# Hybrid decoder step: scan work moved by a step, longer waits on the side chain, and row splits moved beside the second projection

## The chip, the cores and the metric

The kernel runs on one core of a Trainium2 chip. The metric is the device time of one execution in microseconds. The engines are named as the profile names them: PE is TensorE's matmul (PEld its weight load), DVE is VectorE, ACT is ScalarE, POOL is GpSimd, and SP only starts DMAs. One execution of the kernel was profiled; all rows below are from that one.

## What is computed

One step of a hybrid decoder layer: 1024 prompt rows and 8 x 4 sample rows, width 1024. All rows pass one input projection, whose columns feed three branches; the three results (3072 wide) pass one output projection. The reference, cut to the parts that the change touches:

```python
def ssd_scan(x, dt, a, bm, cm, h0):              # branch B, chunks of 128 positions
    acum = jnp.cumsum(dt * a.reshape(SSM_GROUPS, hg), axis=2)
    diff = acum[:, :, :, None] - acum[:, :, None, :]
    decay = jnp.exp(jnp.where(causal, diff, -jnp.inf))
    xdt = x * dt[..., None]
    cb = jnp.einsum('bclgn,bcsgn->bclsg', cm, bm)
    y_diag = jnp.einsum('bclsg,bclsgk,bcsgkp->bclgkp', cb, decay, xdt)
    to_end = jnp.exp(acum[:, :, -1:] - acum)
    chunk_states = jnp.einsum('bclgn,bclgk,bclgkp->bcgkpn', bm, to_end, xdt)
    chunk_decay = jnp.exp(acum[:, :, -1])
    def step(h, inp):
        s_c, d_c = inp
        return h * d_c[..., None, None] + s_c, h
    h_final, h_prev = lax.scan(step, h_init, ...)
    y_off = jnp.einsum('bclgn,bcgkpn,bclgk->bclgkp', cm, h_prev, jnp.exp(acum))
    y = (y_diag + y_off)
    ...
def memory_kv(mem, mem_norm_g, w_mem_k, w_mem_v): # 256 memory rows
    m = rmsnorm(mem, mem_norm_g)
    k = jnp.einsum('bmd,de->bme', m, w_mem_k)
    v = jnp.einsum('bmd,de->bme', m, w_mem_v)
    ...
mixed = jnp.concatenate([a_out, b_out, c_out], axis=-1)
y = x + jnp.einsum('bte,ed->btd', mixed, w_out)
```

The scan's output `y` is gated by SiLU of `z`, normed over each group of 512 columns, and is then branch B's result.

## The kernel before

**Products and the side chain.** Nearly all PE work is products of fp32 data split in two: a high part H, rounded by ACT, and the rest L, subtracted by DVE or POOL (`split`, L120 on). `gemm3` issues three matmuls for each 128-deep piece (L339 to L341) and then calls `hook()`. `hook` adds `pace["rate"]` to a counter and advances the *side chain* (a Python generator, its `yield`s are the steps) whenever the counter passes one. So a rate of 0.56 issues a side step after about every second piece. The instruction streams are written out in the order of these calls; there is no scheduler. Every engine runs its own stream in order.

A *unit* is a 2 x 2 block product of 1024 x 1024 pieces done with seven products (B11, T1, T2, B21, T3, B22, T4); at each product's end DVE combines the result out of PSUM (`u`, `gx`, `go`, L508). PSUM banks for side work come from a ring of four (`sd`, L356).

**Stages in order.** The input projection runs in units; beside the units for q, for the memory gate (`mg`) and for the gMLP gate (`gg`) runs the first side chain: sample convolution, `mem_prep` (norm and transposition of the 256 memory rows), the sample scan, the sample scores and values of the attention, the preparation of gMLP's weights. The `u` units follow. Then come two more units and the first output projection (rows of branch A, added to `y_d`), with the scan of the prompt rows as side chain. Then the *key stage* (L2099 to L2119): sixteen products of the memory rows with the key and value weights. In it the rows of branch B (`yb`) are loaded by SP (`loadB`) and split into `bH`, `bL` (`splitB`). Then the second output projection (`outproj(bH, bL)`) with the attention on the side, and the third.

**The scan.** `scan()` has 16 blocks: two groups g, eight chunks c each, and the state `hT` goes from chunk to chunk. A block has five steps.
1. `sA(i+1)`: for the next block C·B^T and the transposed B (PSUM bank psb), the transposed x, then on DVE `cbm` (masked C·B^T, one buffer), ACT `BH`, DVE `BL`, and `xdt`, `xsD`, `xde`. Then `sE(i+1, 0)`: a product (L1228) of `Lt` and `Rt` gives the exponents of four heads, ACT's Relu and Exp make `MT`.
2. `sNorm`; the state product `pst` (three matmuls, L1273 to L1275: BH, BL, xdH, xdL); the product `po` of the state with C (L1217 to L1219: hH, hL, CH, CL); `sM(i+1, 0)`: `MT` times `cbm` on DVE; `t` on DVE; `hT` times decay on POOL (L1287).
3. Four heads of `pd` (L1292, `MT` with `xdt`); DVE `hT` + `pst` (L1297), `xsD` + `t`; ACT `hH`.
4. Four more heads; `sXsplit(i+1)`: `xdH` on ACT, `xdL` on POOL; `sE(i+1, 1)`, which also calls `r_rows(i + 4)`: a DMA issued by POOL that refills one 32-row quarter of `Rt` from `acc_d`; `sC(i+1)`: `CH` on ACT, `CL` on DVE.
5. Transposition of the block before (`y_T`); `sM(i+1, 1)` on POOL; DVE `xsD` + `pd`, `gate_norm` (DVE, then ACT's Square into `sz`, then POOL's `rstd`, L287 and L288); DVE `hL`; four ACT copies (L1138).

Both decay products read the whole tile `Rt`, so that a refill stands between the reader ahead of it and the next.

**Row splits.** `ytodo` lists the rows (g, c) of branch B; (1, 4) to (1, 7) were kept in SBUF, the others are read from `yb_d`:

```python
    ytodo = [(1, c) for c in range(KEEP, 8)] + [(0, c) for c in range(NTILE)] + [(1, c) for c in range(KEEP)] + [(1, 8)]
    def splitB(lag=1):
        if len(ybs) > lag or (ybs and not ytodo):
```

At most three tiles are open at a time; after each product of the key stage one row tile is split and one loaded, after each fourth product two; what is left at the end is split before the next stage.

Of the kernel before, what the change touches and what calls it, by code (L numbers as in the profile page):

```python
# [19 lines left out]
NTILE = 9  # L20
# [38 lines left out]
def hybrid_step(ctx, tc, x_prompt, x_sample, mem_prompt, state_ssm, state_conv, cache_mem_k,  # L59
# [1161 lines left out]
    def sE(i, j):  # L1221

        s_ = S[i]
        if j == 0:
            s_.MT = []
        s_.MT.append(SC_.p.tile([128, 4, 128], F32, tag="MT", name="MT", bufs=3))
        ps = sd()
        PE.matmul(out=ps, lhsT=Lts[i], rhs=SB_.Rt[:, 4 * j:4 * j + 4, :].rearrange("p h l -> p (h l)"), start=True, stop=True)  # L1228
        if j:
            Lts.pop(i)  # L1230
            r_rows(i + 4)
        E = s_.MT[j].rearrange("p h l -> p (h l)")
        ACT.activation(out=E, in_=ps, func=AF.Relu, scale=-1.0)
        ACT.activation(out=E, in_=E, func=AF.Exp, scale=-1.0)
# [12 lines left out]
    def scan():  # L1247
# [12 lines left out]
        for i in range(16):  # L1260
# [8 lines left out]
            if i > 0:  # L1269
                sNorm(i - 1)  # L1270
                sz_load(i)
            pst = sd()
            PE.matmul(out=pst, lhsT=s_.BH, rhs=s_.xH, start=True, stop=False)  # L1273
            PE.matmul(out=pst, lhsT=s_.BL, rhs=s_.xH, start=False, stop=False)
            PE.matmul(out=pst, lhsT=s_.BH, rhs=s_.xL, start=False, stop=True)  # L1275
            if c > 0:
# [8 lines left out]
            if c > 0:  # L1285
                DVE.tensor_tensor(out=h3(t1), in0=h3(po), in1=hb(ea[:, c, hs], 128, 8), op=ALU.mult)
                POOL.tensor_tensor(out=h3(hT), in0=h3(hT), in1=hb(dec[:, c, hs], 128, 8), op=ALU.mult)  # L1287
            yield
            pd = sd()
            for h in range(8):  # L1290
# [14 lines left out]
            if nx:  # L1305
                sXsplit(i + 1)
                sE(i + 1, 1)
                sC(i + 1)
            yield
            if i > 0:  # L1310
                p = S.pop(i - 1)
                gp_, cp_ = divmod(i - 1, 8)
                r = y_T(p.xsD, 128, gp_, cp_ * 128, acc_bank())
            if nx:
                sM(i + 1, 1)
            DVE.tensor_tensor(out=s_.xsD, in0=s_.xsD, in1=pd, op=ALU.add)
# [7 lines left out]
            if i > 0:  # L1324
                fs.append(y_T2(r, 128, gp_, cp_ * 128, sz))
            yield
            for f in fs:
                f()
# [29 lines left out]
    def sample_scan(sp2):  # L1358
# [87 lines left out]
        def s1(b):  # L1446
            hbt = hb_t.pop(b)
            hTb = [sp2.tile([128, 512], F32, tag="hTb", name="hTb", bufs=3) for _ in range(2)]
            for j in range(2):
                ps = sd()  # L1450
                for i in range(4):
                    PE.transpose(out=ps[:, i * 128:(i + 1) * 128], in_=hbt[:, 4 * j + i, :], identity=ident)
                ACT.activation(out=hTb[j], in_=ps, func=AF.Copy)
            Bm = sp2.tile([96, 2, 128], F32R, tag="Bm", name="Bm", bufs=2)
            POOL.tensor_scalar(out=Bm.rearrange("p g n -> p (g n)"), in0=rb(B3), scalar1=bm3[:, b:b + 1], scalar2=None,
                               op0=ALU.mult)
            for k in range(8):
                ACT.activation(out=hbt[:, k, :], in_=hbt[:, k, :], func=AF.Copy, scale=decT[:, k, b:b + 1])
            St[b] = (hbt, hTb, Bm)

        def s2(b, j):
            hbt, hTb, Bm = St[b]
            if j == 0:
                for g in range(2):
                    PE.matmul(out=accs[32 * g:32 * g + 32, :], lhsT=Cm[:, g, b * 32:(b + 1) * 32],
# [28 lines left out]
        f()  # L1494
        set_pace(1.15)
        sz_s = sp2.tile([128, 8, 128], F32, tag="hb", name="sz_s", bufs=4).rearrange("p k n -> p (k n)")[:32]
# [68 lines left out]
    def sample_scores(sap):  # L1565
# [6 lines left out]
                         in_=qs.rearrange("p k (b t) -> p k b t", t=4))  # L1572
        for _ in range(11):
            yield
# [34 lines left out]
        scores(*prev)  # L1609
        set_pace(1.15)  # L1610
        yield
# [10 lines left out]
    def sample_values(sap):  # L1622
# [26 lines left out]
        DVE.tensor_copy(out=Psm, in_=psO)  # L1649
        set_pace(1.15)  # L1650
        yield
# [13 lines left out]
    def mem_prep(p):  # L1665
# [5 lines left out]
        for i in range(2):  # L1671
            mt = p.tile([128, D], F32, tag="mem", name="mem", bufs=2)
            SP.dma_start(out=mt, in_=mem_prompt[0, i * 128:(i + 1) * 128, :])
            mts.append(mt)
        for _ in range(10):
            yield
        rs = []
        for i in range(2):
# [3 lines left out]
            rs.append(r)  # L1682
            for _ in range(3):
                yield
# [96 lines left out]
    def conv_end():  # L1781
# [3 lines left out]
        pace["acc"] = 0.0  # L1785
        set_pace(1.15)

# [204 lines left out]

    def outproj(H, L):
        units = [(ct, b) for ct in range(8) for b in range(3)]
# [11 lines left out]
        for i, (ct, b) in enumerate(units):  # L2006
            t0, n = TB[b]
            if b == 0:
                (wts[ct],) = w_take(1)
            y_open(i + 1)  # L2010
            ps = gemmA(wts[ct], H, L, t0, n)
            t = yt.pop(i)
# [53 lines left out]
    ybp = yb_ctx.enter_context(tc.tile_pool(name="ybp", bufs=1, side="right"))  # L2066
    ytodo = [(1, c) for c in range(KEEP, 8)] + [(0, c) for c in range(NTILE)] + [(1, c) for c in range(KEEP)] + [(1, 8)]

# [29 lines left out]
    n = 0  # L2098
    for blk in range(8):  # L2099
        wp = w_take(2)  # L2100
        cs = slice((blk % 4) * 256, (blk % 4) * 256 + 256)
        for i in range(2):
# [8 lines left out]
            else:  # L2111
                split(ps[:, :256], vH[:, i, cs], vL[:, i, cs], ACT, DVE)
            splitB()
            loadB()
            if n % 4 == 3:
                splitB()
                loadB()
            n += 1
    side.drain()  # L2119
    while ytodo or ybs:  # L2120
        loadB()
        splitB()
    m_ctx.close()
    yb_ctx.close()
    a_ctx = ExitStack()
# [142 lines left out]
    set_pace(0.43)  # L2268
    outproj(bH, bL)
    side.drain()  # L2270
# [173 lines left out]
```

## Time and profile before

| what | value |
|---|---|
| median of three runs | 1353.83 us (1351.43 to 1354.08) |
| the profiled execution's own time | 1354.25 us |
| its span | 1352.5 us |
| mean granted clock of PE in it | 0.977 |
| busy: PE, PEld | 1284.3 us (95%), 1081.3 us (80%) |
| busy: DVE, ACT, POOL | 754.5 (56%), 586.0 (43%), 349.3 us (26%) |
| DMA | 204.67 MB, mean 151 GB/s |

PE's idle time is about a twentieth of the span; the view of waits lists it by the line that waited and by what ended the wait. The granted clock is given by window: 1.00 is full speed, 0.50 half of it. On the span's scale the memory norm runs around 380 us, the sample steps from 480 to 660, the scan from 785 to 1030, the key stage from 1034 to 1096.

### The profile page before, as it was taken

To read this page: it belongs to the slowest core of one execution; us is meant where nothing else is said; L and a number is where in the kernel's file an instruction comes from. 1 tells how busy PE (TensorE), PEld (TensorE's weight loads), DVE (VectorE), ACT (ScalarE), POOL (GpSimd) and SP (SyncE) were. 2 spreads that over 40 slices of the span, in tenths; PEclk is the share of its full clock that TensorE was granted. 3 is DMA by queue.
4 is the path that set the end of the run, shared out by engine and by line. 5 is a ranking of instruction groups with operands and counts; after the bars stand their busy time and mean duration, and the time that the engine had idled before them with its cause. 6 is when DMAs were issued, how large, how long until landed. Compare 5 with 4: busy or idle time off the path is not lost.

```text
span 1352.5 us, 22010 instructions
## 1 busy us (share of the span) xinstructions
PE 1284.3 (95%) x8211; PEld 1081.3 (80%) x8211; DVE 754.5 (56%) x1258; ACT 586.0 (43%) x1227; POOL 349.3 (26%) x384
## 2 busy tenths in 40 slices
PE   8999999999989989999999978889899889999996
PEld 7999998777867667666788756567678889999996
DVE  6112446999855464433467656776664646653543
ACT  6322333645335633221287545555555533322322
POOL 4400624222543221121145232533230000000122
PEclk9999999999999999999899998899899899999998
DMA  7233331333365556374556565234524876657542
GB/s 239 74 88 95 138 92 42 100 106 108 113 195 158 173 153 224 98 260 128 156 164 188 181 199 160 90 97 130 184 81 149 238 217 202 184 178 257 180 137 99
DMA packets 210621, 204.67 MB, mean 151 GB/s; under 512 B 28124, under 2 KB 176688, under 8 KB 209492
## 3 DMA queue, kind: packets, MB, share of 16 engines
q1 hardware_dynamic: 210004, 203.15, 48.3%
q8 instruction: 65, 1.06, 0.3%
q14 instruction: 40, 0.33, 0.1%
q0 software_dynamic: 512, 0.13, 0.1%
HBM read 138.70 MB, written 64.52 MB: 150 GB/s over the span
## 4 chain that ended last, share of the span: by engine, by line
PE 75%; DVE 8%; DMA 6%; ACT 6%; issue 3%; POOL 1%; SPq 1%; POOLq 0%; ACTq 0%; DVEq 0%
PE ps_mm L339 20%; PE ps_mm L340 18%; PE ps_mm L341 18%; DMA yb<-yb_d 1%; PE ps_acc L1645 1%; PE ps_acc L1583 1%; PE ps_sd L1845 1%; DVE ul L457 1%; PE ps_sd L1598 1%; ACT sz L1138 1%; PE ps_sd L1292 1%; DMA sz<-z_d 1%; DVE xsD L1118 1%; PE ps_sd L317 1%; PE ps_sd L490 1%
## 5 line engine op out<-in xcount | busy, mean ns | idle before, releaser
L449 ACT ACTIVATE uh<-wst 128x512 fp32r<-128x512 f32 x80 | 50.1, 626 | 95.6 <-PE ps_mm L340 89.4
L457 DVE TENSOR_TENSOR ul<-wr,uh 128x512 fp32r<-128x512 f32 x84 | 69.5, 828 | 33.5 <-ACT uh L449 33.5
L2349 POOL TENSOR_TENSOR xres<-xres,gfin 128x1536 f32<-128x1536 f32 (+3 forms) x6 | 14.4, 2397 | 282.8 <-DVE ys L2397 241.7
L127 DVE TENSOR_TENSOR wl<-wr,wh 128x512 fp32r<-128x512 f32 (+3 forms) x53 | 51.1, 987 | 61.5 <-ACT wh L124 60.9
L449 ACT ACTIVATE uh<-wr 128x512 fp32r<-128x512 f32 x84 | 52.4, 624 | 64.6 <-PE ps_mm L340 63.0
L457 DVE TENSOR_TENSOR ul<-wst,uh 128x512 fp32r<-128x512 f32 x80 | 61.1, 764 | 26.4 <-ACT uh L449 26.0
L339 PE MATMUL ps_mm<-bH,wh 128*128 128x384 f32 (+1 forms) x192 | 63.4, 330 | 0.0
L341 PE MATMUL ps_mm<-bH,wl 128*128 128x384 f32 (+1 forms) x192 | 62.1, 323 | 0.0
L340 PE MATMUL ps_mm<-bL,wh 128*128 128x384 f32 (+1 forms) x192 | 62.0, 323 | 0.0
L435 POOL TENSOR_TENSOR wst<-wr 128x512 f32<-128x512 f32 x20 | 26.0, 1299 | 133.1 <-DMA wr<-in_w_in_dram 55.3
L124 ACT ACTIVATE wh<-wr 128x512 fp32r<-128x512 f32 (+3 forms) x60 | 47.0, 814 | 23.2 <-PE ps_mm L340 14.0
L339 PE MATMUL ps_mm<-xB22H,uh 128*128 128x512 f32 x128 | 53.2, 416 | 2.9 <-ACT sz_s L1120 2.1
L1016 DVE SCALAR_TENSOR_TENSOR ps_sd<-raw,vecs,ps_sd 128x512 f32<-128x512 f32 x72 | 54.2, 753 | 1.7
L339 PE MATMUL ps_mm<-xT1H,uh 128*128 128x512 f32 x128 | 53.4, 417 | 0.0
L339 PE MATMUL ps_mm<-xB21H,uh 128*128 128x512 f32 x128 | 53.3, 416 | 0.0
L339 PE MATMUL ps_mm<-xB11H,uh 128*128 128x512 f32 x128 | 52.5, 410 | 0.0
L340 PE MATMUL ps_mm<-xB21L,uh 128*128 128x512 f32 x128 | 51.3, 401 | 0.0
L341 PE MATMUL ps_mm<-xB21H,ul 128*128 128x512 f32 x128 | 51.3, 400 | 0.0
L341 PE MATMUL ps_mm<-xT1H,ul 128*128 128x512 f32 x128 | 50.9, 397 | 0.0
L340 PE MATMUL ps_mm<-xT1L,uh 128*128 128x512 f32 x128 | 50.7, 396 | 0.0
L340 PE MATMUL ps_mm<-xB22L,uh 128*128 128x512 f32 x128 | 50.7, 396 | 0.0
L341 PE MATMUL ps_mm<-xB22H,ul 128*128 128x512 f32 x128 | 50.6, 396 | 0.0
(528 smaller groups left out, 4255.5 us busy)
## 6 DMA issues: line engine op xcount, KB each, us to landing
wr<-in_w_in_dram SPq DMA_DIRECT2D x56, 512.0 KB, 4.1
wr<-in_w_out_dram SPq DMA_DIRECT2D x24, 512.0 KB, 4.9
kv<-in_cache_mem_k_dram SPq DMA_DIRECT2D x16, 512.0 KB, 7.1
kv<-in_cache_mem_v_dram SPq DMA_DIRECT2D x16, 512.0 KB, 4.9
xt<-in_x_prompt_dram SPq DMA_DIRECT2D x8, 512.0 KB, 8.4
z_d<-gt SPq DMA_DIRECT2D x32, 128.0 KB, 1.8
v_d<-gt SPq DMA_DIRECT2D x32, 128.0 KB, 3.7
xc_d<-cd SPq DMA_DIRECT2D x16, 256.0 KB, 2.0
```

Of the source, the lines that this page charges most:

```text
L124: ACT.activation(out=H, in_=raw, func=AF.Copy)
L127: leng.tensor_tensor(out=L, in0=raw, in1=rb(H), op=ALU.subtract)
L317: PE.transpose(out=ps[:, i, :T], in_=self.xn[:T, k * 128:(k + 1) * 128], identity=ident[:T, :T])
L339: PE.matmul(out=ps, lhsT=lH, rhs=rH, start=(first and k == k0), stop=False)
L340: PE.matmul(out=ps, lhsT=lH, rhs=rL, start=False, stop=False)
L341: PE.matmul(out=ps, lhsT=lL, rhs=rH, start=False, stop=(last and k == k0 + kn - 1))
L435: POOL.tensor_tensor(out=t1, in0=A_(u, 2, 1), in1=A_(u, 2, 2), op=ALU.add)
L449: ACT.activation(out=h, in_=src, func=AF.Copy)
L457: eng.tensor_tensor(out=l, in0=src, in1=rb(h), op=ALU.subtract)
L490: PE.matmul(out=ps[32 * j:32 * j + 32, 0:256], lhsT=xs[:, 4 * r + j, :], rhs=R[r][:, j, :], start=(r == 0), stop=(r == 1), tile_position=( ...
L1016: DVE.scalar_tensor_tensor(out=ps, in0=raw[:, 512 * h + j:512 * h + j + 512], scalar=cw(ct, j), in1=ps, op0=ALU.mult, op1=ALU.add)
L2349: eng.tensor_tensor(out=t[:, 0:nf, c0:c0 + w], in0=t[:, 0:nf, c0:c0 + w], in1=gc.unsqueeze(1).to_broadcast([128, nf, w]), op=ALU.mult)
```

## The change

Six edits.
- *Scan, state product.* `pst` moves from the second step to the head of the third; `po` stays in the second.
- *Scan, second decay.* `sC(i+1)` comes right after `sXsplit(i+1)` in the fourth step; `sE(i+1, 1)` moves to the fifth; `sM(i+1, 1)` moves behind it to the start of the next block, behind `rstd` on POOL.
- *Scan, strip rows.* `r_rows` is called in `sE(i, 0)` for block i + 3, and no longer in `sE(i, 1)` for i + 4.
- *Sample scan.* Of eight ACT scalings four move from `s1` to `s2`; the pace between the slow stretches is 1.25, not 1.15, in four places.
- *Waits.* `mem_prep` waits 17 steps for its rows instead of 10, then 5 instead of 3 between the two halves; the scores wait 15 instead of 11.
- *Row splits.* `ytodo` goes by column for the first four columns of both groups. In the key stage the first four products are followed by a load and a split at once; products 4 to 14 by a split of a tile that two others stand behind, and a load; the last by two splits and a load. Four row tiles are split in the second output projection, before its first three units (`b_late`).

```diff
@@ sE
         if j:
             Lts.pop(i)
-            r_rows(i + 4)
+        elif i > 0:
+            r_rows(i + 3)
@@ scan
-            pst = sd()
-            PE.matmul(out=pst, lhsT=s_.BH, rhs=s_.xH, start=True, stop=False)
-            PE.matmul(out=pst, lhsT=s_.BL, rhs=s_.xH, start=False, stop=False)
-            PE.matmul(out=pst, lhsT=s_.BH, rhs=s_.xL, start=False, stop=True)
             if c > 0:
...
             yield
+            pst = sd()
+            PE.matmul(out=pst, lhsT=s_.BH, rhs=s_.xH, start=True, stop=False)
+            PE.matmul(out=pst, lhsT=s_.BL, rhs=s_.xH, start=False, stop=False)
+            PE.matmul(out=pst, lhsT=s_.BH, rhs=s_.xL, start=False, stop=True)
             pd = sd()
...
                 sXsplit(i + 1)
+                sC(i + 1)
+            yield
+            if nx:
                 sE(i + 1, 1)
-                sC(i + 1)
-            yield
             if i > 0:
...
-            if nx:
-                sM(i + 1, 1)
             DVE.tensor_tensor(out=s_.xsD, in0=s_.xsD, in1=pd, op=ALU.add)
...
             yield
+            if nx:
+                sM(i + 1, 1)
             for f in fs:
                 f()
@@ sample scan
-            for k in range(8):
+            for k in range(4):
                 ACT.activation(out=hbt[:, k, :], in_=hbt[:, k, :], func=AF.Copy, scale=decT[:, k, b:b + 1])
...
             if j == 0:
+                for k in range(4, 8):
+                    ACT.activation(out=hbt[:, k, :], in_=hbt[:, k, :], func=AF.Copy, scale=decT[:, k, b:b + 1])
...
-        set_pace(1.15)
+        set_pace(1.25)
@@ sample_scores
-        for _ in range(11):
+        for _ in range(15):
             yield
@@ mem_prep
-        for _ in range(10):
+        for _ in range(17):
             yield
...
-            for _ in range(3):
+            for _ in range(5):
                 yield
@@ row splits
-    ytodo = [(1, c) for c in range(KEEP, 8)] + [(0, c) for c in range(NTILE)] + [(1, c) for c in range(KEEP)] + [(1, 8)]
+    ytodo = ([(1, c) for c in range(KEEP, 8)] + [(g, c) for c in range(4) for g in range(2)] +
+             [(0, c) for c in range(4, NTILE)] + [(1, 8)])
...
-            splitB()
-            loadB()
-            if n % 4 == 3:
-                splitB()
+            if n < 4:
+                loadB()
+                splitB(0)
+            elif n < 15:
+                splitB(2)
+                loadB()
+            else:
+                splitB(0)
+                splitB(0)
                 loadB()
...
-    while ytodo or ybs:
-        loadB()
-        splitB()
     m_ctx.close()
-    yb_ctx.close()
...
-    outproj(bH, bL)
+    def b_late(i):
+        if i < 2:
+            for _ in range(2):
+                splitB(0)
+                loadB()
+        elif i == 2:
+            while ytodo or ybs:
+                loadB()
+                splitB(0)
+            yb_ctx.close()
+    outproj(bH, bL, b_late)
```

What stands on DVE around the memory norm (`xn` is the normed memory row tile, `u`, `gx`, `go` the combinations at a unit's product ends, `ul` low parts of weights). Before:

```order
L457 TENSOR_TENSOR ul<-wr,uh 128x512
L309 SCALAR_TENSOR_TENSOR xn<-mem,rstd,mg_b 128x1024
L481 TENSOR_REDUCE sr<-ps_sd 128x64
L457 TENSOR_TENSOR ul<-wst,uh 128x512
L309 SCALAR_TENSOR_TENSOR xn<-mem,rstd,mg_b 128x1024
L508 TENSOR_TENSOR u<-ps_mm,m_4111 128x512
L508 TENSOR_TENSOR gx<-ps_mm,u 128x512
```

Both norm instructions stand ahead of `u`, which the next product on PE waits for. The same stretch of DVE in the changed kernel:

```order
L457 TENSOR_TENSOR ul<-wr,uh 128x512
L481 TENSOR_REDUCE sr<-ps_sd 128x64
L457 TENSOR_TENSOR ul<-wst,uh 128x512
L508 TENSOR_TENSOR u<-ps_mm,m_4111 128x512
L508 TENSOR_TENSOR gx<-ps_mm,u 128x512
L457 TENSOR_TENSOR ul<-wst,uh 128x512
L309 SCALAR_TENSOR_TENSOR xn<-mem,rstd,mg_b 128x1024
L508 TENSOR_TENSOR go<-ps_mm,m_4111 128x512
L457 TENSOR_TENSOR ul<-wr,uh 128x512
L309 SCALAR_TENSOR_TENSOR xn<-mem,rstd,mg_b 128x1024
```

The norm instructions now stand behind `u` and `gx`.

On ACT one block of the scan reads as follows before (L1233 is the second decay's Relu, L1120 the Square):

```order
L1303 ACTIVATE hH<-hT 128x512
L124 ACTIVATE xdH<-xde 128x512
L1233 ACTIVATE MT<-ps_sd 128x512
L1234 ACTIVATE MT<-MT 128x512
L124 ACTIVATE CH<-bc 128x128
L1120 ACTIVATE sz,ss<-xsD 128x512
```

And in the changed kernel (line numbers are one higher from L1233 on):

```order
L1304 ACTIVATE hH<-hT 128x512
L124 ACTIVATE xdH<-xde 128x512
L124 ACTIVATE CH<-bc 128x128
L1234 ACTIVATE MT<-ps_sd 128x512
L1235 ACTIVATE MT<-MT 128x512
L1120 ACTIVATE sz,ss<-xsD 128x512
```

`CH` moved ahead of the Relu and the Exp.

On POOL one block of the scan before (L955 is the refill of `Rt`, L1238 the second mask product, L287 and L288 `rstd`):

```order
L1287 TENSOR_TENSOR hT<-hT,dec 128x512
L127 TENSOR_TENSOR xdL<-xde,xdH 128x512
L955 DMA Rt<-acc_d 2x1024
L1238 TENSOR_TENSOR MT<-MT,cbm 128x512
L287 TENSOR_SCALAR rstd<-ss 128x1
L288 TENSOR_TENSOR rstd<-rstd,mhalf 128x1
```

And in the changed kernel:

```order
L1284 TENSOR_TENSOR hT<-hT,dec 128x512
L127 TENSOR_TENSOR xdL<-xde,xdH 128x512
L287 TENSOR_SCALAR rstd<-ss 128x1
L288 TENSOR_TENSOR rstd<-rstd,mhalf 128x1
L1239 TENSOR_TENSOR MT<-MT,cbm 128x512
L955 DMA Rt<-acc_d 2x1024
```

The mask product and the refill moved behind `rstd`.

## Rows read from the trace of the kernel before

**Rows 1.** Waits of PE: line waited for; us in total, times, longest.
```profile
PE ps_sd L1217 <- DVE BL L127: 12.3, 9, 2.6
PE ps_sd L1228 <- DMA Rt<-acc_d: 8.0, 3, 4.1
PE ps_mm L339 <- ACT wh L124: 6.7, 2, 3.4
PE ps_mm L339 <- DVE u L508: 4.4, 1, 4.4
...
PE ps_sd L1228 <- ACT sz L1120: 2.3, 1, 2.3
...
PE ps_mm L339 <- ACT sz_s L1120: 2.1, 1, 2.1
PE ps_sd L1598 <- DMA kv<-in_cache_mem_k_dram: 2.1, 1, 2.1
```

**Rows 2.** Windows: us; busy PE, PEld, DVE, ACT, POOL; PEclk; DMA; GB/s.
```profile
385.22:388.62 3.40, 3.40 (x11) 2.72 (x10) 2.07 (x4) 0.17 (x1) 1.69 (x2) 0.50 0.51 167
504.69:508.09 3.40, 3.40 (x22) 1.70 (x21) 1.02 (x2) 1.59 (x4) 0.00 (x0) 0.50 0.97 342
...
sum 27.00, PE 22.51 PEld 14.40 DVE 21.00 ACT 13.84 POOL 8.76; mean PE 4.50 PEld 2.88 DVE 4.20 ACT 2.77 POOL 1.75
...
sum 10.10, PE 8.44 PEld 8.15 DVE 7.77 ACT 7.22 POOL 0.00; mean PE 4.22 PEld 4.07 DVE 3.89 ACT 3.61 POOL 0.00
```

**Rows 3.** Timeline, memory norm: start, us, instruction [idle before, its releaser].
```profile
378.66 1.06 ACT L303 ACTIVATE xn<-mem 128x1024 f32<-128x1024 f32 x1 [4.46 <-DMA mem<-in_mem_prompt_dram]
...
384.92 0.51 PE L339 MATMUL ps_mm<-xT3H,uh 128*128 128x512 f32 x1 [4.44 <-DVE u L508]
```

**Rows 4.** Timeline of one block of the scan, four engines.
```profile
933.85 0.29 DVE L127 TENSOR_TENSOR BL<-ps_sd,BH 128x128 fp32r<-128x128 f32 x1 [1.33 <-ACT BH L124]
...
939.25 1.29 POOL L127 TENSOR_TENSOR xdL<-xde,xdH 128x512 fp32r<-128x512 f32 x1 [4.84 <-ACT xdH L124]
...
941.18 1.28 POOL L1238 TENSOR_TENSOR MT<-MT,cbm 128x512 f32<-128x512 f32 x1
...
941.32 1.29 DVE L127 TENSOR_TENSOR CL<-bc,CH 128x128 fp32r<-128x128 f32 x1 [2.79 <-ACT CH L124]
...
944.57 0.63 ACT L1120 ACTIVATE sz<-xsD 128x512 f32<-128x512 f32 x1 [2.76 <-DVE xsD L1118]
...
945.65 0.56 POOL L288 TENSOR_TENSOR rstd<-rstd,mhalf 128x1 f32<-128x1 f32 x1
...
946.66 0.29 DVE L127 TENSOR_TENSOR BL<-ps_sd,BH 128x128 fp32r<-128x128 f32 x1 [1.33 <-ACT BH L124]
...
947.01 0.51 PE L1217 MATMUL ps_sd<-hH,CH 128*128 128x512 f32 x1 [1.60 <-DVE BL L127]
```

**Rows 5.** Tiles CL and Rt: ns min/median/max, first and last start; us to landing.
```profile
L127 DVE TENSOR_TENSOR CL<-bc,CH x14: 293/1286/1972, 804.1 to 1013.2; 128x128 fp32r<-128x128 f32 x14
...
L955 POOL DMA_DIRECT2D Rt<-acc_d x16: 518/635/803, 780.4 to 953.9; - x16
...
DMA to landing us min/median/max: 1.9/2.3/5.0
```

**Rows 6.** Timeline, key stage: product ends on PE, a split on ACT.
```profile
1039.60 0.27 PE L2091 MATMUL ps_sd<-ident,kst 128*128 128x128 f32 x1
...
1042.69 0.27 PE L2091 MATMUL ps_sd<-ident,kst 128*128 128x128 f32 x1
...
1068.13 0.63 ACT L124 ACTIVATE bH<-yb 128x512 fp32r<-128x512 f32 x1 [4.22 <-DMA yb<-yb_d]
```

**Rows 7.** DMA, 1050 to 1100: GB/s in 40 slices; issues, KB, median us to landing.
```profile
GB/s 174 343 359 308 267 141 262 345 346 304 343 325 325 263 82 14 0 112 311 74 321 354 193 270 141 235 345 329 233 74 12 64 260 169 251 340 275 298 199 297
DMA packets 18974, 11.70 MB, mean 234 GB/s; under 512 B 1646, under 2 KB 18971, under 8 KB 18971
...
yb<-yb_d SPq DMA_DIRECT2D x11, 256.0 KB, 5.4
```

More of the change, by code (lines that the diff above doesn't have):

```diff
@@ L1306, in scan @@
                 sXsplit(i + 1)
-                sE(i + 1, 1)
                 sC(i + 1)
             yield
+            if nx:
+                sE(i + 1, 1)
             if i > 0:
@@ L1609, in sample_scores @@
         scores(*prev)
-        set_pace(1.15)
+        set_pace(1.25)
         yield
@@ L1649, in sample_values @@
         DVE.tensor_copy(out=Psm, in_=psO)
-        set_pace(1.15)
+        set_pace(1.25)
         yield
@@ L1785, in conv_end @@
         pace["acc"] = 0.0
-        set_pace(1.15)
+        set_pace(1.25)
     U.bank = sd
@@ L1991, in hybrid_step, with outproj @@
     TB = [(0, 384), (384, 384), (768, 288)]
-    def outproj(H, L):
+    def outproj(H, L, late=None):
         units = [(ct, b) for ct in range(8) for b in range(3)]
@@ L2010, in outproj @@
             y_open(i + 1)
+            if late is not None:
+                late(i)
             ps = gemmA(wts[ct], H, L, t0, n)
```

## The prediction, on record before the changed kernel ran

> **What bounds the kernel now.** I read the page's first part, then TensorE's idle time by what ended it, then the granted clock in narrow windows, then the timelines of the places found. TensorE (PE) is busy for 95% of the span, so the other engines' shares decide nothing; time can only come out of the rest, and out of stretches in which PE runs at the lower clock. Four places of the change show up. One single idle of 4.4 us is ended by VectorE's `u` (L508), one of 2.1 by the cached keys `kv` and one of 2.1 by `sz_s`; the scan's state-from-C product (L1217) waits 9 times, 12.3 us in all, for `BL`; the scan's decay product (L1228) waits 8.0 us for `Rt` and 2.3 more at a place labelled `sz`; the product that reads the split weight `wh` waits 6.7 us in two idles, both in the memory-key stage [rows 1]. Behind such idles PE runs at half clock: one window of 3.40 us after each of the first two, windows of together 27.00 us in the scan (PE busy for 22.51 of them), and of 10.10 us in the key stage (PE busy 8.44) [rows 2]. At the lower of its two levels (1.2 instead of 2.4 GHz) PE takes twice the time, so half of its busy time there is lost: 1.7 us after each single idle, 11.3 in the scan, 4.2 in the key stage.
>
> **Memory rows wait longer.** VectorE can only reach `u` after the memory norm, which waits for the memory rows' DMA: ScalarE's first pass over `mem` starts at 378.66 after 4.46 us idle, and PE starts again only at 384.92 [rows 3]. Seventeen side steps instead of ten put the two norm instructions behind `u` and `gx` on VectorE; the rows have then landed. Gain 4.4 of idle and 1.7 of clock; I leave 1.0 for the five norm pieces that now meet another unit's end. **−5.1.**
>
> **Sample steps.** Four of eight ScalarE scalings move from one sample step to the next, and the faster pace (1.25 for 1.15) pays for the longer waits, so the side chain ends where it ended, ahead of the `u` units. Waiting 15 steps for the cached keys removes the 2.1 us and its clock window, less 0.5 left over: **−3.3**. The 2.1 us for `sz_s` I expect to find again one unit boundary later: 0. Everything on the side chain is shifted against unit ends; I add **+1** (0 to 3, the upper end being one more idle of the `sz_s` kind with half of its clock).
>
> **Scan, the decay rows.** The DMA that refills `Rt` now goes out at a block's first decay product instead of its second. Both decay products read the tile, so the next reader waits: two steps later before, four steps later now. The DMA lands in 1.9 to 5.0 us, median 2.3 [rows 5]; four steps of a block of 12.8 us in five steps are about 10. It stands on GpSimd behind the second-half mask product now, which costs at most 1.28 us of that. Gone: 8.0 + 2.3 = 10.3 (the last issue starts at 953.9 [rows 5], just ahead of the stretch with the idle called `sz`, whose ScalarE instruction had long ended, so I count that as `Rt`). **−10.3.**
>
> **Scan, the loop through BL.** From one `BL` (933.85) to the next (946.66) a block takes 12.81 us, of which PE idles 1.60 ahead of L1217 [rows 4]; so PE's own work is 11.2 a block, and I take 11.6 as the mean with the blocks that carry a unit's end. Why L1217 waits at all: it needs no `BL`, but its PSUM bank is the one that `BL` must have been read out of. After the change the product that takes that bank a step later is the state product, which needs `BL` anyway. What does the loop cost then? Two things move. (a) `CH` is split right behind `xdH`, ahead of the second decay's Relu; `CL` then ends about with `xdL` (939.25 + 1.29), near 940.8 instead of 942.6: −1.8. (b) The second mask product of GpSimd (1.28 us) now stands behind `rstd`, and `cbm` has one buffer, so VectorE's next `cbm`, with `BL` right behind it, waits for it. From the Square (944.57) `rstd` ends 1.64 later (945.65 + 0.56), the mask product 1.28 after that, and `cbm` and `BL` follow: `BL` starts some 3.1 after the Square instead of 2.09: +1.0. Queued behind the waiting `cbm` are `BL` and the three row products of the next block; the scan's own PE work waits for these. Behind the mask product on GpSimd stands hT*dec, which VectorE's `hT` sum needs a step later. Period 12.81 − 1.8 + 1.0 = 12.0, against 11.6 of PE work: 0.4 left in each of some 12 blocks, 5 of 12.3. **−7.3**, between −2 (0.85 left) and −12.3 (loop below PE's work).
>
> What speaks against (a): `CL`, 0.29 us at its fastest and 1.29 at the median [rows 5], ran beside GpSimd's mask product at 941.18; it now runs beside `xdL`. The trace has the two VectorE rows side by side: `BL`, with one input in PSUM, 0.29; `CL`, with both in SBUF, 1.29 [rows 4]. The Trainium skill ("SBUF — State Buffer", section "Who interferes with whom") says that a VectorE instruction with two SBUF inputs and a GpSimd instruction that reads SBUF share one port pair under a lock, and that whichever comes second blocks fully. The trace agrees. By that rule `CL` cannot end before `xdL`, as (a) has it; without it `CL` would take 0.29 and end a further microsecond earlier, the loop would be near 11.0, below PE's own work, and the time near 1306.
>
> **Scan, the clock.** With 17.6 of some 22.6 us of these idles gone, I give back two thirds of 11.3: **−7.5** (3.8 to 11.3). Scan together −25.1.
>
> **Key stage.** A product takes 3.1 us when nothing waits (1039.60 to 1042.69); ScalarE's split of `bH` waits 4.22 us for a `yb` row, and the next weight's `wh` is behind it on ScalarE [rows 6]. Row loads land in 5.4 us at the median with all the stage's transfers about [rows 7]. Before, a row was split one product after its load; now three lie between, some 9 us. Its first four splits need no load at all (rows kept in SBUF), and the last four go beside the output projection's first three units; nothing there reads these columns before. Gone: 6.7 of idle and 4.2 of clock, **−10.9**. A lower bound is set by the queue: 11.7 MB go through in these 50 us at 234 GB/s on average, with slices of 343 to 359 [rows 7]; in 39 us it would be 300. That fits, with little to spare.
>
> **Sum.** −5.1 − 3.3 + 1 − 10.3 − 7.3 − 7.5 − 10.9 = −43.4, from the profiled execution's own 1354.25 (its span of 1352.5 and what lies around it; 0.4 above the median of the runs): 1311.
>
> **Rivals.**
> 1. *The loop gets no shorter*: `CL` held by `xdL` and `cbm` by the mask product cancel; period still 12.8. For it: both durations are in [rows 4]. Then BL gives 0 and the clock a third: 11.1 worse, 1322. 0.15.
> 2. *Transfers bound the key stage*: the 359 of the best slice can't be held, and idles return as waits for weights. Gain 4 instead of 10.9: 1318. 0.08.
> 3. *The clock stays low where it was*, though the idles shrink (some remain, and these may be enough): 7.5 + 4.2 + 3.4 not given back, 1326. For it: the lower clock already covers far more than the idles themselves. 0.06.
> 4. *Slower: the loop lengthens.* GpSimd's mask product behind `rstd` holds `cbm`, with it `BL` and the state product, whose sum makes the next block's `hH`. One mechanism, in the scan; it decides where it eats what the rest brings with no gain of BL and clock, 5.1 + 3.3 − 1 + 10.3 + 10.9 = 28.6 over 12 blocks: from a period of 12.8 + 2.4 = 15.2. At 15.5 it gives 1358. From 12.0 that takes two and a half more such mask products a block in the loop; against it, one is there. 0.06 (0.04 slower, 0.02 within).
> 5. *The change does not do what it says for `Rt`*: the mask product and queue keep the refill late; 10.3 stays, 1321. 0.03.
> 6. *Better*: the loop falls below PE's work, all clock comes back, the allowances (2.5) aren't needed, and a quarter of some 10 us of other scan waits goes: 5 + 3.8 + 2.5 + 2.5 below, 1297. 0.04.
>
> **Numbers.** My own case 0.58, the rivals 0.42. Its bounds (BL 5 either way, clock 3.8, key stage and shifts a few) and the cases on either side give 1297 to 1327; outside lie rival 4 and the tails. About 0.2%, 2.7 us, is what a measurement here can tell from no change. Faster 0.94, within 0.02, slower 0.04.
>
> **What would show it.** No idle at L1217 ended by `BL`; small idles instead at the state product (after's L1287), ended by `BL`, or at the decay product. No idle ended by `Rt`. `BL` to `BL` about 12.0; if it is over 12.8, steps (a) and (b) are mis-sized and the first rival holds. `CL` ending with `xdL`. The key stage 50 to 52 us long, no `bH` that waits for `yb` over 0.5 us. No idle of 4 us ahead of the product after `u`. Fewer windows at 0.50. Wrong it would be if idles as long come back at the shifted sample steps, or if the splits moved into the output projection hold up its first units.

## The result, and the profile after

The changed kernel takes **1340.96 us** (median of 5 runs, 1338.85 to 1344.90) against 1353.37 for the kernel before; the ratio is 0.9915, with a 95% interval of 0.9893 to 0.9938. It is faster, by 8 to 15 us, and not by the 43 that the sum gave; the forecast of 1311 and its range up to 1327 both missed. The profiled execution took 1339.14 us (span 1337.4), 15.1 less than the one of before.

PE's waits over the whole span of the changed kernel (line waited for; us in total, times, longest):

```profile
PE ps_acc L479 <- ACT sz L1138: 7.7, 2, 5.1
PE ps_sd L1287 <- DVE BL L127: 6.4, 6, 1.8
PE ps_sd L1218 <- DVE hL L1320: 5.2, 3, 2.8
PE ps_mm L339 <- ACT bH L124: 3.8, 2, 2.6
PE ps_mm L339 <- ACT uh L449: 3.2, 2, 2.0
PE ps_mm L339 <- DVE go L508: 3.0, 2, 2.6
PE ps_sd L1411 <- DVE B L127: 2.9, 1, 2.9
PE ps_sd L1228 <- ACT MT L1234: 2.6, 1, 2.6
```

Every wait of [rows 1] is gone or halved: nothing waits for `Rt`, nothing at L1217, nothing for `wh` or the cached keys. In their place stand names that the list before had hardly or not at all. The windows at half clock in the scan (us; busy time of PE, PEld, DVE, ACT, POOL; granted clock, DMA share, GB/s):

```profile
809.43:812.84 3.41, 3.41 (x20) 2.37 (x18) 2.84 (x6) 1.14 (x3) 0.00 (x0) 0.50 0.24 58
...
932.31:935.72 3.41, 3.41 (x9) 2.43 (x9) 1.03 (x3) 2.03 (x7) 3.30 (x5) 0.50 0.39 99
...
sum 27.29, PE 22.23 PEld 14.31 DVE 19.91 ACT 12.59 POOL 11.46; mean PE 3.70 PEld 2.39 DVE 3.32 ACT 2.10 POOL 1.91
```

There are six of them and they add up to 27.29 us, as many as the 27.00 before [rows 2]. (Other executions of the same scan code show less; see the experiments.) The key stage is the opposite: it runs from its first to its last product with PE busy all the time and the clock at 1.00, in 47.8 us; before, from 1033.8 to 1093.7, it took 59.9, 52.5 of them busy. First the window of the changed kernel, then that of the kernel before:

```profile
1026.50:1074.30 47.80, 47.80 (x402) 47.80 (x401) 30.93 (x49) 31.95 (x65) 0.00 (x0) 1.00 0.87 259
```

```profile
1033.80:1093.70 59.90, 52.51 (x402) 51.62 (x401) 34.01 (x54) 34.49 (x70) 0.00 (x0) 0.91 0.75 223
```

Both kernels issue the same 5552 main matmuls (those that write `ps_mm`) in the same order. So the start of each in one trace can be set against its start in the other, and the difference, read at the stages' borders, says where the time went. For the profiled executions (us, minus is faster), worked out from the two traces:

| stage | forecast | measured | of which |
|---|---|---|---|
| to the end of the memory norm | -5.1 | +0.7 | wait for `u` gone; 2.0 for `uh`, 2.9 for `B` new |
| sample scan, scores, values, gMLP preparation | -2.3 | -2.2 | -6.0, then +1.9 and +1.8 |
| scan | -25.1 | -5.8 | |
| key stage | -10.9 | -12.1 | |
| second projection | 0 | +3.1 | waits for `bH` |
| rest | 0 | +1.2 | |

### The profile page after: what moved, and what is told of

Read it like the earlier page. It is cut to its first block, busy times and chain, and to the rows that moved or that the text cites. A ratio compares the mean times of both kernels' runs of the same rounds, so it can differ in the third digit from the quotient of the medians.

```text
span 1337.4 us, 22025 instructions
## 1 busy us (share of the span) xinstructions
PE 1276.8 (95%) x8211; PEld 1075.5 (80%) x8211; DVE 759.7 (57%) x1258; ACT 587.5 (44%) x1227; POOL 348.7 (26%) x384
## 4 chain that ended last, share of the span: by engine, by line
PE 73%; DVE 9%; DMA 8%; ACT 4%; issue 3%; POOL 2%; SPq 1%; POOLq 0%; ACTq 0%; DVEq 0%
PE ps_mm L339 19%; PE ps_mm L341 18%; PE ps_mm L340 18%; DVE ul L457 1%; PE ps_acc L1649 1%; PE ps_acc L1587 1%; DMA yb<-yb_d 1%; PE ps_sd L1849 1%; PE ps_sd L1602 1%; DMA sz<-z_d 1%; DMA y_d<-gt 1%; DMA cr<-c_d 1%; PE ps_sd L317 1%; PE ps_sd L1293 1%; PE ps_acc L490 1%
```

## Experiments

Times are medians; each ratio is against the kernel before, run beside it on the same chip.

**One part at a time.** The three scan edits, `r_rows` alone, the key stage with `b_late`, and the side chain's edits, each put on the kernel before. The edits are those of the diff; `rt_alone` is only:

```diff
-            r_rows(i + 4)
+        elif i > 0:
+            r_rows(i + 3)
```

> The kernel before with the three scan edits alone (state product, second decay, strip rows). Theory A (the prediction's sum): the scan's terms are right and what is missing was lost elsewhere, so about -25 us against the kernel before. Theory B (read from laying the two traces over each other at each main product: the lead of the changed kernel grows from 1.1 to 7.3 us between the scan's first and last product): about -6 us; new waits of PE for hL, MT and the accumulator bank stand where the waits for Rt stood, and as many windows at half clock.

Measured: 1346.35, ratio 0.9956 (0.9940 to 0.9972), some 6 us faster. Theory B held in the time; the scan's gain is missing in the scan itself. As many windows at half clock it did not have: the profiled execution shows 17.07 us of them in the scan, PE busy for 12.12, where the changed kernel's, with the same scan code, showed 27.29 and 22.23. The second of its three windows and their sum:

```profile
858.82:869.05 10.23, 5.55 (x25) 3.36 (x26) 6.99 (x13) 4.88 (x13) 3.90 (x6) 0.50 0.25 71
...
sum 17.07, PE 12.12 PEld 8.59 DVE 10.73 ACT 9.64 POOL 7.71; mean PE 4.04 PEld 2.86 DVE 3.58 ACT 3.21 POOL 2.57
```

> The kernel before, and only the call of r_rows moved to the first decay product. Theory A: the four waits for Rt go and 10.3 us with them. Theory B: beside each of them another thing came late by as much (the gate rows sz, whose DMA holds VectorE and with it hL; the accumulator bank that ScalarE reads), so the idles return under other names: 0 to -4 us, and no wait for Rt in the trace.

Measured: 1350.98, ratio 0.9993 (0.9974 to 1.0012): no difference that can be told from none, where the sum had 10.3. PE's waits in that kernel:

```profile
PE ps_sd L1217 <- DVE BL L127: 16.6, 10, 4.2
PE ps_acc L479 <- ACT sz L1138: 9.6, 2, 7.0
```

No wait for `Rt` is left, and these two have grown from 12.3 [rows 1] and 2.8 us to 16.6 and 9.6: 11.1 us came back under other names for the 10.3 that went. The second of them before:

```profile
PE ps_acc L479 <- ACT sz L1138: 2.8, 2, 2.2
```

The trace of before shows why, at the first of the places. PE comes out of its wait for `Rt` at 837.73, and VectorE is let go at nearly the same time by another transfer, the gate rows `sz`:

```profile
837.73 0.47 PE L1228 MATMUL ps_sd<-Rt,Lt 128*128 128x512 f32 x1 [2.72 <-DMA Rt<-acc_d]
```

```profile
838.16 0.69 DVE L1118 TENSOR_TENSOR xsD<-xsD,sz 128x512 f32<-128x512 f32 x1 [2.42 <-DMA sz<-z_d]
```

Behind that instruction on VectorE stand `hL`, `cbm` and `BL`, which PE needs within the next products. In the changed kernel the same `sz` is all that is left, and PE waits as long at the same place:

```profile
834.03 0.69 DVE L1118 TENSOR_TENSOR xsD<-xsD,sz 128x512 f32<-128x512 f32 x1 [3.32 <-DMA sz<-z_d]
834.64 0.68 DVE L1320 TENSOR_TENSOR hL<-hT,hH 128x512 fp32r<-128x512 f32 x1
```

```profile
835.37 0.50 PE L1218 MATMUL ps_sd<-hL,CH 128*128 128x512 f32 x1 [2.77 <-DVE hL L1320]
```

> The kernel before with the row-split edits alone (order of ytodo, spacing in the key stage, four splits in the second projection). Theory A: -11 us, the key stage some 50 us long, and nothing behind it. Theory B (from the traces): -12 us in the key stage, 3 to 4 given back in the second projection's first three units, where PE waits for bH: -8 us net.

Measured: 1345.17, ratio 0.9943 (0.9924 to 0.9961), 7.7 us faster. Theory B held. The late rows on ScalarE, and the projection's third unit, in the changed kernel:

```profile
1085.13 0.63 ACT L124 ACTIVATE bH<-yb 128x512 fp32r<-128x512 f32 x1 [4.08 <-DMA yb<-yb_d]
1087.07 0.63 ACT L124 ACTIVATE bH<-yb 128x128 fp32r<-128x128 f32 x2 [1.31 <-DMA yb<-yb_d]
```

```profile
1087.43 0.40 PE L339 MATMUL ps_mm<-bH,wh 128*128 128x288 f32 x1 [2.56 <-ACT bH L124]
```

> The kernel before with the side-chain edits alone (memory and score waits, the four scalings, pace 1.25). Theory A: -7.4 us. Theory B: -1 to -2 us: the wait ahead of the product after u goes, but the quicker pace puts ScalarE's sample convolution ahead of a weight split (PE waits 2 us for uh near 371) and a sample product in front of VectorE's wait for a DMA (2.9 us near 403), and the window at half clock only moves.

Measured: 1356.80, ratio 1.0026 (1.0001 to 1.0050): no gain, and rather a loss of 3.5. Both theories had it too good. In the changed kernel ScalarE's convolution step stands one place earlier, ahead of a weight split, and waits there for GpSimd:

```profile
371.90 0.52 ACT L1046 ACTIVATE cvs<-cvs 128x384 f32<-128x384 f32 x1 [8.56 <-POOL cvs L1044]
372.33 1.14 ACT L449 ACTIVATE uh<-wst 128x512 fp32r<-128x512 f32 x2
```

and near 403 VectorE waits 4.69 us for `accTs`, with `B` behind it, which PE needs:

```profile
402.76 2.39 DVE L1394 TENSOR_SCALAR Ls<-accTs 16x32 f32<-16x32 f32 x1 [4.69 <-DMA accTs<-accs_d]
```

In the profiled execution of the edits alone (1363.76 us, the slowest of its ten runs) three windows at half clock follow these idles, where the changed kernel had one (406.66 to 410.07):

```profile
375.41:378.82 3.41, 3.41 (x11) 2.54 (x9) 1.76 (x2) 0.37 (x1) 2.27 (x2) 0.50 0.97 275
409.54:412.95 3.41, 3.41 (x10) 2.62 (x9) 3.41 (x6) 0.63 (x1) 0.00 (x0) 0.50 1.00 300
423.19:426.61 3.42, 3.42 (x14) 2.82 (x13) 0.84 (x2) 1.69 (x5) 0.00 (x0) 0.50 1.10 335
```

**What the scan waits for now.** Of VectorE's waits in the changed kernel's scan (785 to 1030) one stands far above the others:

```profile
DVE cbm L1197 <- POOL MT L1239: 28.5, 13, 2.8
...
DVE xsD L1118 <- DMA sz<-z_d: 6.9, 3, 3.3
```

The first of them in the kernel before:

```profile
DVE cbm L1197 <- POOL MT L1238: 0.3, 1, 0.3
```

One block, on GpSimd and VectorE:

```profile
944.80 0.56 POOL L288 TENSOR_TENSOR rstd<-rstd,mhalf 128x1 f32<-128x1 f32 x1
945.35 1.29 POOL L1239 TENSOR_TENSOR MT<-MT,cbm 128x512 f32<-128x512 f32 x1
```

```profile
934.98 0.29 DVE L127 TENSOR_TENSOR BL<-ps_sd,BH 128x128 fp32r<-128x128 f32 x1 [0.34 <-ACT BH L124]
...
946.67 0.29 DVE L1197 TENSOR_TENSOR cbm<-ps_sd,triu 128x128 f32<-128x128 f32 x1 [2.38 <-POOL MT L1239]
...
947.30 0.29 DVE L127 TENSOR_TENSOR BL<-ps_sd,BH 128x128 fp32r<-128x128 f32 x1 [0.34 <-ACT BH L124]
```

The period from `BL` to `BL` is 12.3 us here; the mask product behind `rstd` holds `cbm`, as step (b) said. Three kernels take up one suspect each, and a fourth the side chain's pace.

```diff
-        s_.cbm = SC_.p.tile([128, 128], F32, tag="cbm", name="cbm", bufs=1)
+        s_.cbm = SC_.p.tile([128, 128], F32, tag="cbm", name="cbm", bufs=2)
```

> The changed kernel with a second buffer for cbm, so that VectorE's next cbm need not wait for GpSimd's mask product behind rstd. In the changed kernel VectorE waits 28.5 us in 13 times there. If that wait sets the loop (the prediction's step b, and the waits of PE for BL that are left, 6.4 us), the time falls by 4 to 7 us against the changed kernel (ratio to the kernel before 0.987 to 0.989 instead of 0.9915). If the loop is set elsewhere (hL behind VectorE's own queue, accumulator bank), the waits of VectorE vanish and the time moves by less than 2 us.

Measured: **1328.00**, ratio 0.9812 (0.9794 to 0.9830), 13 to 14 us better than the changed kernel (by the medians and by the ratios), twice what was expected of it. VectorE's wait is gone from its list, the period falls to 10.7 to 11.2 in five of the blocks, as here:

```profile
926.35 0.29 DVE L127 TENSOR_TENSOR BL<-ps_sd,BH 128x128 fp32r<-128x128 f32 x1 [1.33 <-ACT BH L124]
...
937.54 0.29 DVE L127 TENSOR_TENSOR BL<-ps_sd,BH 128x128 fp32r<-128x128 f32 x1 [1.33 <-ACT BH L124]
```

and the windows at half clock in the scan add up to 20.5 us, within the 17.1 to 27.3 that the scan with one buffer shows. The rest of PE's idle time there stands in few places, two of them at L479.

The second suspect is the pair of `sz` and the accumulator bank. `gate_rows_early` changes the block so:

```diff
-                sz_load(i)
+                if c == 0:
+                    sz_load(i)
...
+                if c < 7:
+                    fy = y_T2(r, 128, gp_, cp_ * 128, SC_.p.tile([128, 512], F32, tag="t1", name="yt", bufs=1))
...
             s_.r = gate_norm(SC_.p, s_.xsD, sz, 128)
+            if c < 7:
+                if i > 0:
+                    fy()
+                sz_load(i + 1)
...
-            if i > 0:
+            if c == 7:
                 fs.append(y_T2(r, 128, gp_, cp_ * 128, sz))
```

> The changed kernel with the four ScalarE copies of the transposed rows moved ahead of the Square and written to the tile t1 instead of sz, and the next block's load of sz issued right behind the Square (in seven of eight blocks), so that it waits for no store and no copy. Theory B: the two things that took the place of Rt go: the accumulator waits (L479, 7.7 us in two) and VectorE's waits for sz (6.9 us in three, with them most of PE's 5.2 us for hL): 6 to 10 us faster than the changed kernel, and up to two windows at half clock fewer. Rival: the loop through VectorE takes it up again, under 3 us.

Measured: 1337.35, ratio 0.9875 (0.9857 to 0.9893), 4 to 5 us better than the changed kernel, between the theory and the rival. The edit takes up both suspects at once, so which of the two brought it is not shown. In PE's waits in its scan (785 to 1030) next to nothing is left at L479, and many small waits for `BL` stand there instead, since the loop is still held by `cbm`:

```profile
PE ps_sd L1288 <- DVE BL L127: 10.6, 11, 1.8
...
PE ps_acc L479 <- ACT yt L1138: 0.7, 2, 0.5
```

The third takes the four kept rows out of `ytodo`, splits one after each of the first four products of the key stage, and issues a load beside each, so that the last three of fourteen loaded tiles are split after the last product.

> The changed kernel with three row loads issued beside the splits of the kept rows, so that all fourteen loaded tiles are split inside the key stage and none in the second projection. If the late splits cost what the traces show (PE waits 3.8 us for bH in the projection's first three units), 3 to 4 us faster than the changed kernel. If the queue of transfers is what limits the key stage, the waits move back into it and the time stays within 1 us or rises.

Measured: 1340.23, ratio 0.9904 (0.9888 to 0.9920). Against the changed kernel that is not clear of the runs' spread. In its profiled execution the projection's first units wait for no `bH`, and the stretch from 1031 to the end is 3 us shorter than in the changed kernel's.

> The changed kernel with the side chain's first pace at 1.15 again (the three later ones stay at 1.25, the waits stay long). If it is the quicker pace that puts the sample convolution's ScalarE step ahead of the weight split and the sample product ahead of its DMA, the idles of 2.0 us (near 371) and 2.9 us (near 403) go, some 5 us with the half-clock window behind them. Rival: other steps then meet the same boundaries, and the later end of the side chain costs as much: within 2 us.

Measured: 1345.93, ratio 0.9942 (0.9928 to 0.9956): 4 to 5 us worse than the changed kernel. The rival held, and more: the two idles go, but the slower chain ends later and meets the gMLP preparation at other places (the stretch from 640 to 700 costs 9 us more than before, against 2 with the quicker pace).

**Which scan edit lost it, and do the causes add?** First, GpSimd's mask product ahead of `rstd` again, with one buffer:

```diff
+            if nx:
+                sM(i + 1, 1)
             DVE.tensor_tensor(out=s_.xsD, in0=s_.xsD, in1=pd, op=ALU.add)
...
             yield
-            if nx:
-                sM(i + 1, 1)
```

> The changed kernel with GpSimd's second mask product ahead of rstd again, as in the kernel before, and one buffer for cbm; everything else as changed. The run with two buffers says that cbm's wait cost 13 us. If that wait is the whole of it, putting the mask product ahead of rstd should bring nearly the same, 10 to 13 us against the changed kernel (ratio 0.981 to 0.984). If the second buffer helped for another reason (a freer order on VectorE), this brings less than 4 us.

Measured: 1334.92, ratio 0.9865 (0.9825 to 0.9906), with runs from 1329 to 1344. The median gain of 6 to 7 us is only half of the expected; its profiled execution is 10 us below the changed kernel's, and within the scan it gains 17.4 us on the kernel before, as two buffers do (18.0). The two ways of freeing `cbm` are alike in the scan. PE's mean granted clock goes part of the way with the spread of the runs: 0.984 and 0.985 in the two near 1329, 0.974 in the slowest (1344.46), but 0.984 in one at 1336.22 too.

> The kernel before, and only the state product moved to the head of the third step. The prediction's reading: L1217 waited because its PSUM bank is the one that BL is read out of; then these waits (12.3 us in 9) leave L1217 and a smaller wait stands at the state product, 3 to 7 us faster. Rival: the wait goes with BL to the state product in full and nothing is gained, within 2 us.

Measured: 1348.74, ratio 0.9962 (0.9942 to 0.9983), 5 us faster, as the prediction's reading had it. The waits for `BL` fall from 12.3 to 2.2:

```profile
PE ps_sd L1228 <- DMA Rt<-acc_d: 14.0, 5, 4.5
...
PE ps_sd L1286 <- DVE BL L127: 2.2, 3, 1.2
```

and the waits for `Rt` grow from 8.0 (10.3 with the place labelled `sz`) to 14.0.

> The kernel before, and only the second decay with its mask product moved a step later and CH ahead of it; one buffer for cbm. If the wait of cbm for the mask product behind rstd is what ate the scan's gain, this edit by itself costs time: the period from BL to BL grows to 13 or more, 3 to 10 us slower than before. If CH's gain and cbm's wait cancel, as the prediction's first rival had it, within 2 us.

Measured: 1350.09, ratio 0.9977 (0.9962 to 0.9992), 3 us faster. That misses both, though VectorE waits for the mask product here too:

```profile
DVE cbm L1197 <- POOL MT L1238: 24.4, 11, 3.3
```

Beside it stand the waits of PE of the old loop, 12.8 us for `BL` and 13.0 for `Rt`. That the mask product costs little beside these, and becomes the limit only once they are gone, is argued from these lists; no run gives this kernel a second buffer.

> The three scan edits on the kernel before, with a second buffer for cbm and nothing else. If cbm's wait was the loss inside the scan, about 12 us better than the scan edits alone (ratio 0.9956): 0.986 to 0.988. If the gain of the second buffer needed the other edits, less than 5 us better.

Measured: 1336.19, ratio 0.9873 (0.9851 to 0.9896): 17 to 18 us faster than before, 11 better than the scan edits with one buffer. The loss sits in the scan and needs none of the other edits.

Last, all three fixes together, with the changed kernel's side chain, with that of the kernel before, and with its two offending steps moved (two steps more ahead of the convolution's ScalarE step, two fewer in the memory wait, three more ahead of `Ls`).

> The changed kernel with all three: two buffers for cbm, gate rows early, row splits early. If the three causes are separate the gains add: 13 + 4 + 1 to 3 us, ratio 0.976 to 0.979. If the gate rows and the mask product waited for the same thing, no better than the two buffers alone, 0.981.

Measured: **1315.74**, ratio 0.9711 (0.9680 to 0.9741): by the ratios 28 us better than the changed kernel, where the single gains (14, 5 and 1.5) add up to 21. With the intervals of all five ratios these 7 us are not clear of the spread, but the scan stage of the profiled executions says the same: it is 33.8 us shorter than before, against 5.8 in the changed kernel, 18.0 with two buffers and 14.7 with the gate rows early, so 28 for the fixes together and 12 and 9 for two of them alone. Each alone had left the others' waits in place. In the scan one window at half clock is left (3.41 us).

> As three_fixes, but with the side chain's waits, scalings and pace as in the kernel before. Alone, the side-chain edits took 3.5 us more than they gave. If that holds beside the others, this is 2 to 4 us faster than three_fixes. If the edits are only neutral and the single run of them met half-clock windows by chance, the two differ by less than 2 us.

Measured: 1312.47, ratio 0.9701 (0.9674 to 0.9727). 1 to 3 us better than the former, with intervals that overlap: the side-chain edits bring nothing, and whether they cost a little is open.

> As three_fixes, with two side steps more ahead of ScalarE's sample convolution and two fewer in the memory wait, and three more ahead of VectorE's step that reads accTs. If the two idles near 371 (2.0 us) and 403 (2.9 us) come from these steps standing one place too early, both go, 4 to 6 us less than three_fixes with the clock window near 406. Rival: the later steps meet other unit ends, no gain.

Measured: **1308.79**, ratio 0.9679 (0.9649 to 0.9708), the lowest median of all, 4 to 7 us below three_fixes, with intervals that overlap. The idles of 2.0 and 2.9 us are gone; one of 3.3 ahead of the product after `u` came instead, the window at half clock near 410 stayed, and another of 6.83 us (420.65 to 427.48) came behind it. So the two profiled executions are level up to 430 and differ by 1.2 us at the end: the expected gain did not come where it was expected, and where that of the medians sits is not shown.

## Why the prediction was wrong

The direction was right. Of 43.4 us that the sum gave, 28 did not come in the profiled execution; by its own steps:

- **`Rt`, -10.3: the step that failed.** It took the whole of each wait as gain because its releaser would come early, and did not ask what is late next at the same place. With the early refill alone PE idles for 16.0 us at the four places, where it had idled for 14.7 (4.16 for 2.72; 7.02 for 4.07 and 2.22 close behind; 2.18 for 1.21 and 1.52; 2.60 for 2.32 and 0.62). At the first, `sz` held VectorE, and through it `hL` and `BL`. At the second and the fourth the Square, which stands on ScalarE ahead of the four copies that free the accumulator bank, waited for VectorE's `xsD`, and at the third it was `BL` again. Alone the edit gave 0.9 us (from 3.5 gained to 1.6 lost, by the interval). The fourth place, labelled `sz`, was counted as `Rt` in disguise; with `Rt` early, 2.6 us remain there, at L479. No run takes the early refill out of the kernel with the three fixes, so what it is worth there is open.
- **The clock in the scan, -7.5: mis-sized, and one execution does not settle by how much.** In the profiled execution nothing came back: idles of 1.9 to 5 us remained, and the half-clock time was 27.3 us for 27.0. That is the third rival for the scan, to which 0.06 was given. But three other profiled executions with the same scan code have 17.1 us (the scan edits alone), 20.5 (the early row loads) and 20.5 (the first pace as before), with PE busy for 12.1 to 15.5 us of it instead of 22.2, so that some 3.4 to 5 us came back there, half of the difference, by the prediction's own reckoning. Clearly lower it is with the gate rows early (10.2 us) and in the three kernels with all the fixes (3.4, 6.8 and 6.8); two buffers alone (20.5, and 23.9 beside the old side chain) do not show it.
- **The loop through `BL`, -7.3: right in mechanism, mis-sized in step (b).** PE's waits for `BL` fell by 5.9 us, but the loop got hardly shorter. Step (a) came as written: `CL` ends 6.8 us after `BL` in the block shown above, where it had ended 8.8 after it [rows 4], so 2.0 where 1.8 were priced. Step (b) was seen and priced at 1.0 and measured 1.5: `BL` starts 3.6 us after the Square, in nearly every block, instead of 2.1 before and the 3.1 of the sum. The sum left out `BH`: in the changed kernel's trace `BH` on ScalarE waits for `cbm`, and `BL` for `BH`. On ScalarE, in that block:

```profile
943.72 0.63 ACT L1120 ACTIVATE sz<-xsD 128x512 f32<-128x512 f32 x1 [1.32 <-DVE xsD L1118]
...
946.99 0.28 ACT L124 ACTIVATE BH<-ps_sd 128x128 fp32r<-128x128 f32 x1 [1.38 <-DVE cbm L1197]
```

Its period is 12.3 against the 12.0 of the sum. On the mean of the ten blocks that take between 10 and 15 us it is 12.9, for 13.0 before, and two of them went from 12.4 and 11.5 to 14.0 (in one of these VectorE waits 2.95 us for `sz`). With two buffers the `BL` of most blocks starts 2.1 us after the Square again and the mean is 11.6, which is what the sum had put for PE's own work: 13 to 14 us that the change left lying. As to (a), `CL` now runs beside `xdL`, and in none of 14 blocks under 1.27 us, where its fastest had been 0.29 [rows 5]. The tile `CL` in the changed kernel (ns, min/median/max):

```profile
L127 DVE TENSOR_TENSOR CL<-bc,CH x14: 1272/1282/1936, 800.9 to 1005.6; 128x128 fp32r<-128x128 f32 x14
```

That is the lock that the Trainium skill describes ("SBUF — State Buffer", section "Who interferes with whom"); the trace agrees: in 13 of the 14 blocks `CL` ends some 0.15 us behind `xdL`.
- **Key stage, -10.9: right** (-12.1), with no idle and the full clock as forecast, at 259 GB/s. What it said of the late splits fell short: nothing reads these columns before they are split, but the units right behind do, and the second projection's first units were held up, by 3.1 us. The prediction had named that as what could make it wrong, and priced it at nothing.
- **Memory rows, -5.1: failed.** The 4.4 us wait for `u` went as described, but the quicker pace moved steps that the prediction had not followed onto places where they wait: 2.0 us for `uh`, 2.9 for `B`, and the half-clock window came 21 us later instead of not at all. The +1 set aside for such shifts was too small; that stretch alone cost 5.8 more than forecast.
- **Sample steps, -3.3 and +1: right in sum** (-2.2), but by luck, with larger terms on both sides: -6.0 in the scores, +1.9 and +1.8 behind them. A second window at half clock went there (487.61 to 491.02 before) that the prediction had not counted, and an idle of 2.6 us for `go` came.

So 19 of the 28 us were lost in the scan, 6 at the memory norm, 4 behind the key stage, which itself gave 1 more than forecast. The fourth rival, a longer loop, named the mechanism that did the harm (`cbm` behind the mask product), but on the mean it did not lengthen the loop; it kept it from getting shorter, which is what the first rival (0.15) had.

## What to carry to other kernels

A wait that is removed is worth what is left until the next thing at the same place, so before the sum takes a stall as gain, look for other engines that were let go at about the same time. In a loop of several engines, a tile with one buffer that two of them share is a link of the loop, and moving one reader later can cost most of what the move brings (1.5 of 2.0 us a block here); a second buffer of 512 bytes a partition brought as much here as the whole change had (13 to 14 us, and 8 to 15). A quicker pace or a longer count of steps moves everything behind it on a side chain, and each moved step has to be looked at against what it will wait for there.

## What the runs showed of the hardware

The clock's answer to an idle is not fixed. Seven kernels with the same side-chain edits have the same two idles (2.0 and 2.9 us); between 370 and 430 the profiled executions of six of them show one window at 0.50 and that of `side_alone` three. And the same scan code shows 17.1 to 27.3 us at 0.50 in four executions. Runs of the changed kernel lie 6 us apart (1338.85 to 1344.90), those of `side_alone` 12, with the same instructions; in the latter the mean granted clock falls as the time grows (0.981 at 1351.68 us, 0.974 at 1363.76). These 0.007 of the span are some 9 of the 12 us, which is an estimate. In the scan, fixes made together gave more than the sum of each alone (28 us in its stage against 12 and 9); that the half-clock time fell with them, from 27.3 us to 3.4, is measured, that this is the whole of the difference is not.
